# The first projection unit computed directly from x as it lands, sums of x formed in place by VectorE, cache copies issued in the FFN

## The chip, the cores and the metric

The kernel runs on one core of a Trainium2 chip. The metric is device time in microseconds of one execution of the whole program. Before the change the median of three runs is 2027.93 us (2026.84 to 2028.01). The engines named in the rows are PE (TensorE matmuls) and PEld (TensorE weight loads), DVE (VectorE), ACT (ScalarE), POOL (GpSimd) and SP (SyncE, which issues the DMAs).

## The reference, cut to what matters

One layer of a decoder trunk: a prompt of 1024 rows and 8 sample rows go through the same weights. All branches begin with one projection of x, and at the end stands a SwiGLU.

```python
z = x @ w_in
xr, yr, q, k, v, xq, g = jnp.split(z, SPLIT_IDX, axis=-1)
xc, conv_new = causal_conv(xr, conv_buf, conv_w, conv_b)
hs, h_new = rg_lru(xc, h0, lru_wa, lru_ba, lru_wx, lru_bx, lru_lambda)
a_out = hs * jax.nn.gelu(yr, approximate=True)
...
s_out, wk_new, wv_new = swa_decode(q, k, v, win_k, win_v, sinks)
c_out = mem_attn(xq.reshape(B, T, N_XHEADS, XHEAD_DIM), mem_k, mem_v)
gates = jax.nn.sigmoid(g.reshape(B, T, N_BRANCH, D_MODEL) + b_gates)
merged = sum(gates[:, :, n] * (br @ w_branch[n]) for n, br in enumerate((a_out, s_out, c_out)))
h = layer_norm(ALPHA * x + merged @ w_out, ln1_g, ln1_b)
gt, up = jnp.split(h @ w_gate_up, 2, axis=-1)
h = layer_norm(ALPHA * h + (jax.nn.silu(gt) * up) @ w_down, ln2_g, ln2_b)
```

`wk_new` and `wv_new` are the window caches of the sample rows: 127 old rows of each of 8 caches and one new row. The kernel makes the old rows' part by two copies from DRAM to DRAM, o_swk and o_swv.

## The kernel before, in words

**Layout.** Activations are held transposed: features on the 128 partitions, 1032 columns of rows (1024 of the prompt, 8 of the sample). Every matmul is exact to nearly f32 by a split: a value is written as hi plus lo, both in the fp32r type, and a product is three matmuls (hi by hi, hi by lo, lo by hi). The split of a tile is one cast on ACT (line 71, or 77 with a factor) and one subtraction on DVE (line 72, or 78).

**The projection.** 30 units, listed in UNITS ("xq" 0, "lru" 0, "gate" 0, "xq" 1, "lru" 1, ...), each make two blocks of 128 columns of z. A unit is computed by a Strassen-Winograd scheme: the 2 by 2 blocks of weights (two column blocks, two halves of D) and the 2 by 2 blocks of x (two halves of D, two halves of the rows) are combined into seven products instead of eight. Each product i is done for two halves p of its columns, 258 columns each, over 4 k steps with 3 matmuls each, so a unit is 168 matmuls. In the rows u_ih and u_il are hi and lo of the weight operand of product i, th and tl those of the x operand; products 0, 2, 4 and 6 go to the bank ub, 1 and 5 to ud, 3 to uc. The sums of weights (us, line 228) and their splits are made per unit by `fast_quarter`. The seven x operands are the same for all units and are made once, by `combos` (lines 161 to 208), while unit 0 runs: blocks of x are loaded one after the other (x<-xQ, eight DMAs of 516 KB), the four combinations for p = 0 are formed by DVE and those for p = 1 by POOL (line 180), each into a tile of its own, and all seven are split. Product i of unit 0 can start when operand i is ready.

`project` (lines 287 to 323) walks through all products of all units, calls `fast_quarter` three products ahead, and after each product `pump`, which moves side work one step on: the decode cross-attention of the sample rows (`dec_mem`, one per xq unit, pumped at every second call) and the lru branch. `dec_mem` loads tiles dck of the memory keys (two buffers) and the broadcast queries dcq (two buffers), multiplies and reduces them on DVE (dcj, line 757), and later sums values with the weights (dcv, dcw, line 781). It starts from `Finish.done` of its xq unit, which scales z, splits it (za, zb, hi_xq, lines 336 and 337) and stores it. The lru side work casts the convolved rows (xc to xch and xcl, lines 71 and 72) and runs small gate matmuls (g, lines 105 to 107).

**The cache copies.** `dec_win_scores`, late in the projection's program text, issues o_swk and o_swv (lines 809 to 811). A scheduler places them at build time; in the trace they are issued at 29 and 60 us.

**The FFN.** For each block f of 128 hidden columns, gate weights wfg and up weights wfu are loaded in two halves each (wfg3r, wfu3r: raw halves of block 3; line 82), split by ACT and DVE, and multiplied in three column chunks c = 0, 1, 2 (384, 384 and 264 columns) into fg and fu. Then ft = tanh(fg/2), ft = (ft + 1) fg, ft = ft fu (line 1041), and ft is split into gH and gL.

**What sets the order.** The program is a sequence of calls; a list scheduler at build time fixes one order of instructions for each engine from its own estimates of durations, and inserts the semaphore waits. On the chip each engine takes its instructions strictly in that order, so an instruction that waits holds up everything behind it on its engine. `tc.issue_after(x)` makes a DMA stand behind instruction x. Tile pools give the buffers out in turn: z has 9 buffers of 128 x 1032, "t" 28 buffers for x operands, "qh" 5 for weight his.

Of the kernel before, what the change touches and what calls it, by code (L numbers as in the profile page):

```python
# [10 lines left out]
F32 = mybir.dt.float32  # L11
F32R = mybir.dt.float32r
AF = mybir.ActivationFunctionType
ALU = mybir.AluOpType
# [4 lines left out]
P = 128  # L19
D = 1024  # L20
# [3 lines left out]
T = TP + NB  # L24
# [8 lines left out]
BANKS = {"mm": 3, "s": 2, "t": 2, "o": 1}  # L33
HT = T // 2
QN = T // 4
QS = 272
UNITS = (
    ("xq", 0), ("lru", 0), ("gate", 0), ("xq", 1), ("lru", 1), ("gate", 1), ("xq", 2), ("lru", 2), ("gate", 2),
    ("xq", 3), ("lru", 3), ("gate", 3), ("k", 0), ("lru", 4), ("v", 0), ("q", 0), ("lru", 5), ("gate", 4),
# [14 lines left out]
class Builder:  # L54
# [89 lines left out]


    def zt(self, name):
        return self.z.tile([P, T], F32, tag="z", name=name, bufs=9)

    def x_quarter(self, kh, th, p):

# [1 line left out]
        self.x_loaded = self.nc.sync.dma_start(t, self.io["xQ"][kh, 2 * th + p]).ins  # L152
        return t

    def combos(self, load, quarter):


        nc = self.nc
        ts = [[None] * 7, [None] * 7]
        for i in reversed(range(7)):  # L160
            for p in range(2):
                ts[p][i] = tuple(self.tp.tile([P, 4, QS], F32R, tag="t", name=f"t{e}{i}_{p}", bufs=28) for e in "hl")
        raw, t = [{}, {}], [{}, {}]

        def keep(i, p, src, sign=1.0):
            hi, lo = (a[:, :, :QN] for a in ts[p][i])
# [6 lines left out]
        def fetch(*where):  # L173
            for p in range(2):
                for kh, th in where:
                    raw[p][kh, th] = self.x_quarter(kh, th, p)

        def both(op, name, p, a, b):
            t[p][name] = self.zt(f"{name}_{p}")
            (nc.gpsimd if p else nc.vector).tensor_tensor(t[p][name], a, b, op)  # L180

        load(0)
        quarter(0)
        fetch((0, 0))
        for p in range(2):
            keep(0, p, raw[p][0, 0])
        load(1)
        quarter(1)
        fetch((0, 1))
        for p in range(2):  # L190
            both(ALU.subtract, "t1", p, raw[p][0, 0], raw[p][0, 1])
            keep(1, p, t[p]["t1"])
        fetch((1, 1))
        quarter(2)
        for p in range(2):
            both(ALU.subtract, "t3", p, raw[p][1, 1], raw[p][0, 1])
            both(ALU.add, "t2n", p, t[p]["t3"], raw[p][0, 0])
            keep(2, p, t[p]["t2n"], -1.0)
        load(3)
        fetch((1, 0))  # L200
        for p in range(2):
            keep(3, p, raw[p][1, 0])
        for p in range(2):
            keep(4, p, t[p]["t3"])
            keep(5, p, raw[p][1, 1])
            both(ALU.subtract, "t4", p, t[p]["t2n"], raw[p][1, 0])
            keep(6, p, t[p]["t4"])
        return ts

    def fast_load(self, u, src0, src1):  # L210
# [77 lines left out]
    def project(self):  # L288

        nc, io, tc = self.nc, self.io, self.tc  # L290
        self.qdc = self.cst.tile([P, KT * NB], F32, name="qdc")
        self.qds = self.cst.tile([P, KT * NB], F32, name="qds")
        self.kd = self.cst.tile([P, 2 * NB], F32, name="kd")
        self.vd = self.cst.tile([NB, 256], F32, name="vd")
        self.lru_setup()
        self.side, self.pumped = (deque(), deque()), 0
        n = len(UNITS)
        finish = [Finish(self, kind, j) for kind, j in UNITS]
        st = {}

        def load(u):
            a, b = finish[u].rows
            st[u] = self.fast_load(u, io["win"][a], io["win"][b])
            if u:
                st[u]["load"]((0, 0), (0, 1), (1, 0), (1, 1))

        load(0)
        parts = {0: ((0, 0),), 1: ((1, 0), (1, 1)), 3: ((0, 1),)}
        ts = self.combos(lambda i: st[0]["load"](*parts[i]), lambda i: self.fast_quarter(st[0], i))
# [491 lines left out]
    def dec_win_scores(self):  # L801

        nc, io, dp = self.nc, self.io, self.dp
        krow = dp.tile([NB, 256], F32, tag="krow", name="krow", bufs=1)
        ps = self.bank("mm", "dkt")
        for m in range(2):
            nc.tensor.transpose(ps[:NB, m * P:(m + 1) * P], self.kd[:, m * NB:(m + 1) * NB], self.ident)
        nc.scalar.copy(krow, ps[:NB, :256])
        for name, cache, row in (("o_swk", "cwk", krow), ("o_swv", "cwv", self.vd)):
            with self.tc.issue_after(self.last_mm):  # L810
                nc.sync.dma_start(io[name][:, 0:P - 1, :], io[cache][:, 1:P, :])
# [218 lines left out]
    def ffn(self, h):  # L1030
        nc, io, ph = self.nc, self.io, self.ph

        def gate_up(f, c, wg, wu, j):
            t0, n = CH[c]
            pg = self.mm_tile(wg, h, c, f"fg{f}_{c}", tag=("s", "t")[c % 2])
            self.norm_step()
            t = ph.tile([P, 384], F32, tag="gt", name=f"ft{f}_{c}", bufs=3)[:, :n]
            nc.scalar.activation(t, pg, AF.Tanh, scale=0.5)  # L1038
            nc.vector.scalar_tensor_tensor(t, t, 1.0, pg, op0=ALU.add, op1=ALU.mult)  # L1039
            pu = self.mm_tile(wu, h, c, f"fu{f}_{c}")  # L1040
            nc.vector.tensor_mul(t, t, pu)  # L1041
# [236 lines left out]
```

## Time and profile before

| | before |
|---|---|
| median of 3 runs | 2027.93 us |
| profiled execution, its span | 2027.6 us |
| PE busy in the span | 1963.3 us (97%), 13732 matmuls |
| DVE busy | 1204.2 us (59%) |
| ACT busy | 879.1 us (43%) |
| POOL busy | 125.3 us (6%) |
| DMA | 235.41 MB, mean 116 GB/s |
| mean granted TensorE clock | 0.991 |
| first 50 us: PE busy, granted clock | 29.98 us, 0.86 |
| 50 to 130 us: PE busy, granted clock | 71.81 us, 0.96 |

The profile is of one execution; its own time is the span, 2027.6 us, 0.3 us under the median. A row of the timeline reads: start, duration, engine, line, operation, output from inputs, count, and in brackets how long the engine had been idle before it and what released it. Matmul durations overlap, since matmuls are pipelined; the distance between starts is the pace.

### The profile page before, as it was taken

To read this page: it belongs to the slowest core of one execution; us is meant where nothing else is said; L and a number is where in the kernel's file an instruction comes from. 1 tells how busy PE (TensorE), PEld (TensorE's weight loads), DVE (VectorE), ACT (ScalarE), POOL (GpSimd) and SP (SyncE) were. 2 spreads that over 40 slices of the span, in tenths; PEclk is the share of its full clock that TensorE was granted. 3 is DMA by queue.
4 is the path that set the end of the run, shared out by engine and by line. 5 is a ranking of instruction groups with operands and counts; after the bars stand their busy time and mean duration, and the time that the engine had idled before them with its cause. 6 is when DMAs were issued, how large, how long until landed. Compare 5 with 4: busy or idle time off the path is not lost.

```text
span 2027.6 us, 35380 instructions
## 1 busy us (share of the span) xinstructions
PE 1963.3 (97%) x13732; PEld 1930.0 (95%) x13732; DVE 1204.2 (59%) x2565; ACT 879.1 (43%) x1922; POOL 125.3 (6%) x164
## 2 busy tenths in 40 slices
PE   6899999999999999999999999999999999999997
PEld 5899999999999898988999999999999999999996
DVE  8597888777676555389886568533322332223357
ACT  5456565555656455388774244422201221122324
POOL 3000010100000000012110003100000000000001
PEclk8999999999999999999999999999999999999999
DMA  4365455462333676567525241111211111111102
GB/s 173 129 227 181 153 186 170 144 228 82 118 131 114 234 240 215 158 170 204 155 72 174 85 145 30 43 42 43 58 47 43 42 57 41 57 45 43 56 28 84
DMA packets 140439, 235.41 MB, mean 116 GB/s; under 512 B 17280, under 2 KB 69584, under 8 KB 140240
## 3 DMA queue, kind: packets, MB, share of 16 engines
q1 hardware_dynamic: 140272, 233.17, 36.2%
q8 instruction: 107, 1.75, 0.4%
q14 instruction: 60, 0.49, 0.1%
HBM read 179.95 MB, written 55.23 MB: 116 GB/s over the span
## 4 chain that ended last, share of the span: by engine, by line
PE 86%; DVE 6%; DMA 3%; ACT 3%; issue 1%; SPq 0%; ACTq 0%; DVEq 0%; POOL 0%; POOLq 0%
PE ub L245 5%; PE ub L244 5%; PE ub L246 5%; PE fg L105 4%; PE fg L106 4%; PE fg L107 4%; PE fu L107 4%; PE fu L105 4%; PE fu L106 4%; PE d L105 3%; PE d L107 3%; PE d L106 3%; PE ud L246 2%; PE ud L245 2%; PE ud L244 2%; PE brs L105 1%
## 5 line engine op out<-in xcount | busy, mean ns | idle before, releaser
L105 PE MATMUL fg<-hH,wfg_h 128*128 128x384 f32 (+1 forms) x528 | 168.3, 319 | 3.0 <-DVE acc L1012 1.7
L106 PE MATMUL fg<-hL,wfg_h 128*128 128x384 f32 (+1 forms) x528 | 167.7, 318 | 0.4 <-DVE hL L1023 0.4
L107 PE MATMUL fu<-hH,wfu_l 128*128 128x384 f32 (+1 forms) x528 | 167.7, 318 | 0.0
L106 PE MATMUL fu<-hL,wfu_h 128*128 128x384 f32 (+1 forms) x528 | 167.6, 317 | 0.0
L105 PE MATMUL fu<-hH,wfu_h 128*128 128x384 f32 (+1 forms) x528 | 167.5, 318 | 0.0
L107 PE MATMUL fg<-hH,wfg_l 128*128 128x384 f32 (+1 forms) x528 | 167.5, 317 | 0.0
L1041 DVE TENSOR_TENSOR ft<-ft,fu 128x384 f32<-128x384 f32 (+1 forms) x66 | 33.8, 513 | 139.1 <-PE fu L107 139.1
L105 PE MATMUL d<-gH,wd_h 128*128 128x384 f32 (+1 forms) x360 | 114.4, 318 | 0.0
L106 PE MATMUL d<-gL,wd_h 128*128 128x384 f32 (+1 forms) x360 | 114.2, 317 | 0.0
L107 PE MATMUL d<-gH,wd_l 128*128 128x384 f32 (+1 forms) x360 | 114.2, 317 | 0.0
L1039 DVE SCALAR_TENSOR_TENSOR ft<-ft,fg 128x384 f32<-128x384 f32 (+1 forms) x66 | 33.8, 513 | 135.2 <-ACT ft L1038 132.9
L71 ACT CAST gH<-ft 128x384 fp32r<-128x384 f32 (+1 forms) x66 | 31.7, 481 | 175.0 <-DVE ft L1041 175.0
L105 PEld LDWEIGHTS fg<-hH,wfg_h 128*128 128x128 f32 x528 | 99.1, 188 | 3.9 <-DVE acc L1012 2.0
L106 PEld LDWEIGHTS fg<-hL,wfg_h 128*128 128x128 f32 x528 | 99.2, 188 | 1.0 <-DVE hL L1023 0.9
L107 PEld LDWEIGHTS fg<-hH,wfg_l 128*128 128x128 f32 x528 | 99.3, 188 | 0.0
L107 PEld LDWEIGHTS fu<-hH,wfu_l 128*128 128x128 f32 x528 | 99.2, 188 | 0.0
L105 PEld LDWEIGHTS fu<-hH,wfu_h 128*128 128x128 f32 x528 | 99.2, 188 | 0.0
L106 PEld LDWEIGHTS fu<-hL,wfu_h 128*128 128x128 f32 x528 | 99.2, 188 | 0.0
L1061 DVE SCALAR_TENSOR_TENSOR acc<-d,acc 128x384 f32<-128x384 f32 (+1 forms) x48 | 24.8, 516 | 108.4 <-PE d L107 108.4
L1038 ACT ACTIVATE ft<-fg 128x384 f32<-128x384 f32 (+1 forms) x66 | 30.1, 456 | 134.8 <-PE fg L107 134.8
L244 PE MATMUL ub<-th,u_0h 128*128 128x258 f32 x240 | 69.4, 289 | 7.5 <-ACT th L71 6.1
L244 PE MATMUL ud<-th,u_1h 128*128 128x258 f32 x240 | 70.2, 293 | 6.3 <-ACT u_1h L71 5.2
(957 smaller groups left out, 6872.4 us busy)
## 6 DMA issues: line engine op xcount, KB each, us to landing
ur<-win SPq DMA_DIRECT2D x120, 256.0 KB, 3.6
dck<-cmk SPq DMA_DIRECT2D x32, 256.0 KB, 3.6
dcv<-cmvT SPq DMA_DIRECT2D x32, 256.0 KB, 4.5
st<-scr_q SPq DMA_DIRECT2D x32, 256.0 KB, 5.2
scr_g<-za SPq DMA_DIRECT2D x12, 516.0 KB, 5.8
scr_g<-zb SPq DMA_DIRECT2D x12, 516.0 KB, 3.7
x<-xQ SPq DMA_DIRECT2D x8, 516.0 KB
scr_a<-ge SPq DMA_DIRECT2D x8, 516.0 KB
```

The lines of the kernel that those rows point to most:

```text
L71: ins = self.nc.scalar.copy(hi, src).ins
L105: nc.tensor.matmul(ps, sh, mh, start=i == 0, stop=False)
L106: nc.tensor.matmul(ps, sh, ml, start=False, stop=False)
L107: self.last_mm = nc.tensor.matmul(ps, sl, mh, start=False, stop=closes and i == last).ins
L244: mm(sh[:, w], xh, start=opens and k == 0, stop=False)
L245: mm(sh[:, w], xl, start=False, stop=False)
L246: self.last_mm = mm(sl[:, w], xh, start=False, stop=k == 3).ins
L1038: nc.scalar.activation(t, pg, AF.Tanh, scale=0.5)
L1039: nc.vector.scalar_tensor_tensor(t, t, 1.0, pg, op0=ALU.add, op1=ALU.mult)
L1041: nc.vector.tensor_mul(t, t, pu)
L1061: nc.vector.scalar_tensor_tensor(a, ps, 0.5, a, op0=ALU.mult, op1=ALU.add)
```

## The change

**The first unit.** Unit 0 is no longer done by seven products. `begin` takes the place of `combos`. It loads the unit's weights undivided (four halves), and the eight blocks of x in the order in which they are needed, and computes z of unit 0 block by block: for each quarter of the rows (th, p) it splits the two blocks of x of that quarter and multiplies them by both column blocks, 4 times 48 = 192 matmuls into the banks ub ("mm") and ud ("t"), which ACT then copies to za and zb.

**The x operands.** The splits of three blocks of x, made for unit 0, are used again as operands 0, 3 and 5 of the later units. The other four are formed in place, in the tiles of x, by DVE for p = 0 and p = 1 (three `change` calls in `begin` before operands 1 and 2, one before operand 6, for each p); POOL forms none. The z pool has 10 buffers instead of 9, and the "t" tiles 264 columns a row instead of 272.

**What follows.** `finish.done` of unit 0 (its scaling, split and store, and the start of its `dec_mem`) is called from `begin`; the seven-product units are 1 to 29.

**The cache copies.** o_swk and o_swv leave `dec_win_scores` and are issued in the FFN, behind the load of wfu of block 2 and of block 4.

```diff
-QS = 272
+QS = 264
...
-        return self.z.tile([P, T], F32, tag="z", name=name, bufs=9)
+        return self.z.tile([P, T], F32, tag="z", name=name, bufs=10)
...
-    def combos(self, load, quarter):
...
-        def both(op, name, p, a, b):
-            t[p][name] = self.zt(f"{name}_{p}")
-            (nc.gpsimd if p else nc.vector).tensor_tensor(t[p][name], a, b, op)
...
+    def begin(self, rows, finish, load_next, next_quarter):
...
+        def weight(j, e):
+            raw = self.half_raw(io["win"][rows[j]][:, e * h:(e + 1) * h], h, f"ur0_{j}{e}")
+            if e == 0:
+                w[j] = [None, None, pair(f"w{j}")]
+            flat = [a.rearrange("p k n -> p (k n)")[:, e * h:(e + 1) * h] for a in w[j][2]]
+            w[j][e] = flat
+            return lambda: self.split(*flat, raw)
...
+        def quarter(th, p, z):
+            tags = ("mm", "t")
+            for kh in range(2):
+                xh, xl = (a[:, :, :QN] for a in hl[kh, th, p])
+                for j in range(2):
+                    if kh == 0:
+                        ps[j] = self.bank(tags[j], f"u0{th}{p}{j}")[:, :QN]
+                    wh, wl = w[j][kh]
+                    for k in range(4):
+                        c, first, last = slice(k * P, (k + 1) * P), kh + k == 0, kh == 1 and k == 3
+                        nc.tensor.matmul(ps[j], wh[:, c], xh[:, k, :], start=first, stop=False)
+                        nc.tensor.matmul(ps[j], wh[:, c], xl[:, k, :], start=False, stop=False)
+                        self.last_mm = nc.tensor.matmul(ps[j], wl[:, c], xh[:, k, :], start=False, stop=last).ins
+            for j in range(2):
+                nc.scalar.copy(z[j][:, cols(th, p)], ps[j])
+
+        def change(op, p, to, a, b):
+            nc.vector.tensor_tensor(x[(*to, p)], x[(*a, p)], x[(*b, p)], op)
+            return x[(*to, p)]
...
+        for th, p in ((0, 1), (1, 0), (1, 1)):
+            block(0, th, p)
+            block(1, th, p)
+            quarter(th, p, z)
+            if (th, p) == (1, 0):
+                load_next()
+                next_quarter(0)
         for p in range(2):
...
+            ts[p][0], ts[p][3], ts[p][5] = hl[0, 0, p], hl[1, 0, p], hl[1, 1, p]
+            change(ALU.subtract, p, (1, 1), (1, 1), (0, 1))
+            ts[p][1] = keep(f"1_{p}", change(ALU.subtract, p, (0, 1), (0, 0), (0, 1)))
+        next_quarter(1)
         for p in range(2):
...
+            ts[p][2] = keep(f"2_{p}", change(ALU.add, p, (0, 0), (1, 1), (0, 0)), -1.0)
+        next_quarter(2)
+        finish.done(*z)
         for p in range(2):
...
+            ts[p][4] = keep(f"4_{p}", x[1, 1, p])
         for p in range(2):
...
+            ts[p][6] = keep(f"6_{p}", change(ALU.subtract, p, (1, 0), (0, 0), (1, 0)))
         return ts
...
-        todo = [(u, i) for u in range(n) for i in range(7)]
+        todo = [(u, i) for u in range(1, n) for i in range(7)]
...
-        for name, cache, row in (("o_swk", "cwk", krow), ("o_swv", "cwv", self.vd)):
-            with self.tc.issue_after(self.last_mm):
-                nc.sync.dma_start(io[name][:, 0:P - 1, :], io[cache][:, 1:P, :])
+        for name, row in (("o_swk", krow), ("o_swv", self.vd)):
             nc.sync.dma_start(io[name][:, P - 1, :], row)
...
+                if f in (2, 4):
+                    name, cache = (("o_swk", "cwk"), ("o_swv", "cwv"))[f // 2 - 1]
+                    with self.tc.issue_after(self.last_load):
+                        nc.sync.dma_start(io[name][:, 0:P - 1, :], io[cache][:, 1:P, :])
```

The scheduler's orders of the two programs differ on PE, DVE and ACT in the first ten or so units of the projection, and in the FFN only around blocks 3 and 5. Three places matter below. In these rows a tile has its number behind its name, and a line number counts in its own program (72 is in both the subtraction of a split).

The first place is DVE while operands of x are made. Before, in unit 0, the combinations of p = 0 (line 180) stand between the splits of operands (tl) and of unit 0's weights (u_4l, u_5l):

```order
L180 TENSOR_TENSOR t_0_184<-x_174,x_162 128x1032
L72 TENSOR_TENSOR u_4l<-us_4_304,u_4h 128x512
L180 TENSOR_TENSOR t2n_186<-t_0_184,x_144 128x1032
L228 TENSOR_TENSOR us_5_340<-us_2_178,ur_01_196 128x512
L228 TENSOR_TENSOR us_1_438<-ur_10_300,ur_11_302 128x512
L78 SCALAR_TENSOR_TENSOR tl_0_127<-t2n_186,th_0_126 128x4x258
L72 TENSOR_TENSOR u_5l<-us_5_340,u_5h 128x512
L78 SCALAR_TENSOR_TENSOR tl_1_129<-t2n_192,th_1_128 128x4x258
L180 TENSOR_TENSOR t_0_210<-t2n_186,x_198 128x1032
L72 TENSOR_TENSOR tl_0_123<-x_198,th_0_122 128x4x258
```

Now, behind the scaling of unit 0's z, the last sums in place (line 204) and the splits of operands 4 and 6 stand ahead of the first weight split of unit 1's product 3 (u_3l); nsnk and lruc are small constants:

```order
L72 TENSOR_TENSOR tl_0_447<-x_132,th_0_446 128x4x258
L72 TENSOR_TENSOR tl_1_451<-x_136,th_1_450 128x4x258
L204 TENSOR_TENSOR x_122<-x_114,x_122 128x1032
L204 TENSOR_TENSOR x_128<-x_126,x_128 128x1032
L72 TENSOR_TENSOR tl_0_456<-x_122,th_0_455 128x4x258
L72 TENSOR_TENSOR tl_1_461<-x_128,th_1_460 128x4x258
L660 TENSOR_SCALAR lruc<-vec 128x8
L72 TENSOR_TENSOR u_3l<-ur_01_330,u_3h 128x512
L789 SCALAR_TENSOR_TENSOR dcj_0_0_550,dcs_545<-dck_0_548,dcq_0_546 128x256
L789 SCALAR_TENSOR_TENSOR dcj_0_1_552,dcs_545<-dck_0_548,dcq_0_546 128x256
L263 TENSOR_TENSOR us_4_562<-ur_00_328,ur_10_332 128x512
```

What moved: the sums of p = 1, which POOL made before, now stand on DVE beside those of p = 0 (x_122 and x_128 here are the two for operand 6), and u_3l stands behind them and behind all splits of x.

The second place is DVE at the start of the unit behind the first lru unit. Before, the splits of the lru rows (xcl_1, xcl_2) and four products of the decode attention (dcj) stand ahead of the unit's first weight sums (us_1, us_2) and of u_1l:

```order
L72 TENSOR_TENSOR xcl_1_1054<-xc_792,xch_1_1053 128x344
L276 TENSOR_TENSOR za_943<-ud_0_854,u2s_0_904 128x258
L72 TENSOR_TENSOR xcl_2_1188<-xc_792,xch_2_1187 128x344
L757 SCALAR_TENSOR_TENSOR dcj_0_0_685,dcs_521<-dck_0_683,dcq_0_681 128x256
L757 SCALAR_TENSOR_TENSOR dcj_0_1_687,dcs_521<-dck_0_683,dcq_0_681 128x256
L757 SCALAR_TENSOR_TENSOR dcj_0_0_754,dcs_521<-dck_0_752,dcq_0_681 128x256
L757 SCALAR_TENSOR_TENSOR dcj_0_1_756,dcs_521<-dck_0_752,dcq_0_681 128x256
L228 TENSOR_TENSOR us_1_1021<-ur_10_844,ur_11_846 128x512
L228 TENSOR_TENSOR us_2_1057<-us_1_1021,ur_00_840 128x512
L72 TENSOR_TENSOR u_1l<-us_1_1021,u_1h 128x512
```

Now us_1 and us_2 of that unit, and u_0l and u_1l, stand ahead of xcl_1 and xcl_2:

```order
L263 TENSOR_TENSOR us_1_1003<-ur_10_826,ur_11_828 128x512
L263 TENSOR_TENSOR us_2_1047<-us_1_1003,ur_00_822 128x512
L789 SCALAR_TENSOR_TENSOR dcj_0_0_1043,dcs_545<-dck_0_1041,dcq_0_1039 128x256
L263 TENSOR_TENSOR us_4_1141<-ur_00_822,ur_10_826 128x512
L72 TENSOR_TENSOR u_0l<-ur_00_822,u_0h 128x512
L789 SCALAR_TENSOR_TENSOR dcj_0_1_1131,dcs_545<-dck_0_1127,dcq_0_1039 128x256
L308 SCALAR_TENSOR_TENSOR zb_971<-ub_1_805,p5s_1_864 128x258
L72 TENSOR_TENSOR u_1l<-us_1_1003,u_1h 128x512
L263 TENSOR_TENSOR us_5_1181<-us_2_1047,ur_01_824 128x512
L72 TENSOR_TENSOR xcl_1_1036<-xc_776,xch_1_1035 128x344
L72 TENSOR_TENSOR xcl_2_1178<-xc_776,xch_2_1177 128x344
```

What moved is us_1, us_2 and u_1l: from behind both splits of lru rows to ahead of both.

The third place is ACT in the FFN at the passage from block 2 to block 3 (the passage from 4 to 5 reads alike). Before, three of the four casts of block 3's weights (wfg_h, wfu_h of wfg3r and wfu3r) stand ahead of the cast of block 2's last chunk (gH_2), and the fourth, not shown, still further ahead:

```order
L71 CAST gH_1_16734<-ft_1_16705 128x384
L71 CAST wfg_h<-wfg3r__16802 128x512
L71 CAST wfu_h<-wfu3r__16808 128x512
L1038 ACTIVATE ft_2_16763<-fg_2_16738 128x264
L71 CAST wfu_h<-wfu3r__16814 128x512
L71 CAST wfg_h<-wfg4r__16994 128x512
L71 CAST gH_2_16792<-ft_2_16763 128x264
L1038 ACTIVATE ft_0_16845<-fg_0_16820 128x384
```

Now all four stand behind it:

```order
L71 CAST gH_1_16723<-ft_1_16694 128x384
L1068 ACTIVATE ft_2_16752<-fg_2_16727 128x264
L71 CAST gH_2_16781<-ft_2_16752 128x264
L71 CAST wfg_h<-wfg3r__16785 128x512
L71 CAST wfg_h<-wfg3r__16791 128x512
L71 CAST wfu_h<-wfu3r__16797 128x512
L71 CAST wfu_h<-wfu3r__16803 128x512
L71 CAST wfg_h<-wfg4r__16983 128x512
L1068 ACTIVATE ft_0_16834<-fg_0_16809 128x384
```

The casts wfg3r and wfu3r moved from ahead of gH_2 of block 2 to behind it, together with the first cast of block 4.

More of the change, by code (lines that the diff above doesn't have):

```diff
@@ L153, in x_quarter, with keep @@
         return t
-    def combos(self, load, quarter):
[L158 to L166, printed above, removed]
+    def begin(self, rows, finish, load_next, next_quarter):
+        nc, io, h = self.nc, self.io, D // 2
+        pair = lambda name: tuple(self.tp.tile([P, 4, QS], F32R, tag="t", name=f"t{e}{name}", bufs=28) for e in "hl")
+        x, hl, ts, w, ps = {}, {}, [[None] * 7, [None] * 7], [[None] * 2, [None] * 2], {}
+        cols = lambda th, p: slice(HT * th + QN * p, HT * th + QN * (p + 1))
+        def weight(j, e):
[5 more added lines that the diff above has]
+            return lambda: self.split(*flat, raw)
+        def keep(name, src, sign=1.0):
+            tiles = pair(name)
+            hi, lo = (a[:, :, :QN] for a in tiles)
             src = src.rearrange("p (k n) -> p k n", k=4)
@@ L171, in keep, with fetch @@
                 self.split(hi, lo, src)
[L173 to L176, printed above, removed]
-        def both(op, name, p, a, b):
-            t[p][name] = self.zt(f"{name}_{p}")
[L180 to L184, printed above, removed]
+            return tiles
+        def fetch(kh, th, p):
+            x[kh, th, p] = self.x_quarter(kh, th, p)
@@ new lines, in block @@
+        def block(kh, th, p):
+            hl[kh, th, p] = keep(f"{kh}{th}{p}", x[kh, th, p])
+        def quarter(th, p, z):
[13 more added lines that the diff above has]
+                nc.scalar.copy(z[j][:, cols(th, p)], ps[j])
@@ new lines, in change @@
+        def change(op, p, to, a, b):
+            nc.vector.tensor_tensor(x[(*to, p)], x[(*a, p)], x[(*b, p)], op)
+            return x[(*to, p)]
+        s00 = weight(0, 0)
+        fetch(0, 0, 0)
+        s10, s01 = weight(1, 0), weight(0, 1)
+        fetch(1, 0, 0)
+        s11 = weight(1, 1)
+        for th, p in ((0, 1), (1, 0), (1, 1)):
+            fetch(0, th, p)
+            fetch(1, th, p)
+        z = self.zt("za0"), self.zt("zb0")
+        s00()
+        block(0, 0, 0)
+        s10()
@@ L185, in combos @@
+        s01()
+        block(1, 0, 0)
+        s11()
+        quarter(0, 0, z)
+        for th, p in ((0, 1), (1, 0), (1, 1)):
+            block(0, th, p)
[4 more added lines that the diff above has]
+                next_quarter(0)
         for p in range(2):
[L186 to L189, printed above, removed]
+            ts[p][0], ts[p][3], ts[p][5] = hl[0, 0, p], hl[1, 0, p], hl[1, 1, p]
+            change(ALU.subtract, p, (1, 1), (1, 1), (0, 1))
+            ts[p][1] = keep(f"1_{p}", change(ALU.subtract, p, (0, 1), (0, 0), (0, 1)))
@@ L199, in combos @@
-        load(3)
-        fetch((1, 0))
-        for p in range(2):
[L202 to L207, printed above, removed]
+            ts[p][4] = keep(f"4_{p}", x[1, 1, p])
+        for p in range(2):
+            ts[p][6] = keep(f"6_{p}", change(ALU.subtract, p, (1, 0), (0, 0), (1, 0)))
         return ts
@@ L303, in load @@
             st[u] = self.fast_load(u, io["win"][a], io["win"][b])
[L304 to L309, printed above, removed]
+            st[u]["load"]((0, 0), (0, 1), (1, 0), (1, 1))
+        ts = self.begin(finish[0].rows, finish[0], lambda: load(1), lambda i: self.fast_quarter(st[1], i))
         with tc.issue_after(self.x_loaded):
```

7 lines of the change are left out of this document (removed).

## The prediction

> **What bounds the kernel now.** I read the page first, then the windows of the stages that the change touches, then PE's waits there.
>
> ```profile
> PE 1963.3 (97%) x13732; PEld 1930.0 (95%) x13732; DVE 1204.2 (59%) x2565; ACT 879.1 (43%) x1922; POOL 125.3 (6%) x164
> 0.00:50.00 50.00, 29.98 (x182) 28.07 (x183) 43.57 (x62) 24.87 (x38) 17.27 (x16) 0.86 0.48 172
> 50.00:130.00 80.00, 71.81 (x559) 69.83 (x558) 53.62 (x136) 38.45 (x77) 0.32 (x2) 0.96 0.53 177
> 130.00:680.00 550.00, 543.64 (x4482) 541.28 (x4480) 422.55 (x833) 310.43 (x586) 33.09 (x39) 1.00 0.45 152
> 1290.00:1400.00 110.00, 110.00 (x707) 110.00 (x707) 36.14 (x66) 26.31 (x52) 0.05 (x1) 1.00 0.17 51
> ```
>
> In a window row stand the window, its length, busy us of PE, PEld, DVE, ACT, POOL with their instructions, PE's granted clock, DMA share and GB/s. PE is the bound with 97% of 2027.6 us; of its 64 us of idle time 20 lie in the first 50 us and 8 in the next 80, and only there is the granted clock below 1. DVE is busy for 43.57 of the first 50 us. In the FFN (the last row) PE has no gap at all: there the change can only lose. PE's waits in the first 130 us:
>
> ```profile
> PE ub L244 <- ACT th L71: 6.1, 1, 6.1
> PE ub L244 <- ACT th L77: 5.4, 1, 5.4
> PE ud L244 <- ACT u_1h L71: 5.2, 2, 4.5
> DVE xcl L72 <- ACT xch L71: 8.7, 3, 7.2
> DVE dcj L757 <- DMA dck<-cmk: 2.8, 3, 1.2
> ```
>
> (Total, times, longest.) The first 6.1 are the start, which stays. The 5.4 are unit 0 waiting for operand 2, which needs two sums of blocks. The longest of the 5.2 lies in unit 3 and answers to the last two rows, DVE's own waits: DVE stood 7.2 us for a row of lru work while the weights of unit 3 were queued behind it.
>
> **Paces.**
>
> ```profile
> 7.72 0.42 PE L246 MATMUL ub<-th,u_0l 128*128 128x258 f32 x1
> 11.38 0.37 PE L245 MATMUL ub<-tl,u_0h 128*128 128x258 f32 x1
> 16.73 0.58 PE L245 MATMUL ud<-tl,u_1h 128*128 128x258 f32 x1 [3.06 <-DVE tl L72]
> 36.13 0.39 PE L245 MATMUL uc<-tl,u_3h 128*128 128x258 f32 x1 [1.38 <-DVE tl L72]
> 36.48 0.28 PE L244 MATMUL uc<-th,u_3h 128*128 128x258 f32 x1
> 39.95 0.28 PE L246 MATMUL ud<-th,u_5l 128*128 128x258 f32 x1
> 68.72 0.28 PE L244 MATMUL ub<-th,u_0h 128*128 128x258 f32 x1
> 124.70 0.28 PE L244 MATMUL ub<-th,u_0h 128*128 128x258 f32 x1
> 144.98 0.28 PE L244 MATMUL ub<-th,u_0h 128*128 128x258 f32 x1
> ```
>
> From 7.72 to 11.38 are 17 steps of 0.215 us: cold. From 36.48 to 39.95 are 29 steps of 0.1197: warm. A cold spell lasts about 20 matmuls, 4.3 us, and costs 20 x 0.095 = 1.9 us. After 1.38 us of idle time (36.13) PE was warm; 3.06 (16.73) left it cold. The last three rows are the first matmuls of units 2, 4 and 5.
>
> **(a) Units 0 and 1: -10.8.** Before, they end at 68.72. After, the first two matmuls hang on the same first loads and casts; I keep 6.07 for the first and 7.34 for the second. The other 190 of the 192 are 20 x 0.215 + 170 x 0.12 = 24.7, so unit 0 ends at 32.0, if x comes in time:
>
> ```profile
> 0.00:16.00 16.00, 5.85 (x25) 5.15 (x25) 9.77 (x12) 8.32 (x11) 2.85 (x5) 0.97 0.84 312
> ```
>
> 312 GB/s over 16 us are 5.0 MB; unit 0 wants 8 x 516 KB and 4 x 256 KB, 5.2 MB, there by 16.8 us at that rate. The last two blocks are wanted when quarter 3 begins at 26.3, less 2.3 for cast and split: slack of some 7 us. Unit 1 then runs products 0 to 2 (72 matmuls, 8.6 us, and 0.3 for the small transposes of unit 0's decode columns) to 40.9, and wants u_3l of product 3. In the first order fence that stands behind the sums and splits of x on DVE. Its price:
>
> ```profile
> 18.94 3.43 DVE L180 TENSOR_TENSOR t<-x,x 128x1032 f32<-128x1032 f32 x1
> 18.50 2.78 POOL L180 TENSOR_TENSOR t<-x,x 128x1032 f32<-128x1032 f32 x1 [4.12 <-DVE tl L72]
> 26.80 0.68 DVE L228 TENSOR_TENSOR us<-ur,ur 128x512 f32<-128x512 f32 x1
> 37.53 1.23 DVE L72 TENSOR_TENSOR tl<-x,th 128x1032 fp32r<-128x1032 f32 x1
> 38.68 1.22 DVE L72 TENSOR_TENSOR tl<-t,th 128x1032 fp32r<-128x1032 f32 x1
> ```
>
> A full-width row of DVE takes 1.23 and starts 1.15 after the last (37.53 to 38.68); a row of 512 goes at 0.60. Beside POOL's sum the same work took 3.43; with POOL without sums I take 1.15. The last block of x is split at about 21.3: its cast stands on ACT behind the copy of quarter 1's first bank, at 19.1. From there DVE has, up to and with u_3l, 17 full-width rows (8 of them sums in place), 6 weight rows and 5 small ones of 0.08: 19.6 + 3.6 + 0.4 = 23.6, so 44.9. PE stands 3.5 to 4 us, long enough to go cold, and has 92 matmuls left: 20 x 0.215 + 72 x 0.12 = 12.9. Unit 1 ends at 57.9: -10.8.
>
> Bounds: without the stall 52.3 (-16.4). On the other side the first products of the decode attention (dcj) stand on DVE right behind u_3l and wait for dcq:
>
> ```profile
> 53.58 0.35 SPq L740 DMA_DIRECT2D dcq<-drow_c  x1
> 57.98 0.80 SPq L751 DMA_DIRECT2D dcq<-dcq  x2
> dcq<-dcq SPq DMA_DIRECT2D x16, 256.0 KB, 3.4
> ```
>
> 4.4 us from issue to issue and 3.4 to land: unit 0's z is split by 36.9, the issue comes at 37.6, dcq lands at 45.4, when DVE arrives. If it is late by 3.5, unit 1's u_4l and u_5l are late too: 61.5 (-7.2).
>
> **(b) Units 2 and 3: -12.5.** From 68.72 to 124.70 are 55.98 us; unit 4, undisturbed, takes 144.98 - 124.70 = 20.28. What fills the rest:
>
> ```profile
> 97.61 0.52 DVE L72 TENSOR_TENSOR xcl<-xc,xch 128x344 fp32r<-128x344 f32 x1 [7.23 <-ACT xch L71]
> L105 PE MATMUL g<-xch,wgh 128*128 128x344 f32 x6 | 2.1, 356 | 0.7 <-ACT xch L71 0.7
> dck<-cmk SPq DMA_DIRECT2D x32, 256.0 KB, 3.6
> ```
>
> xcl_2 (97.61) needs a cast that ACT makes behind the eviction of unit 3's product 0; behind xcl_2 stand us_1, us_2 and u_1l, without which product 1 cannot start. In the second order fence these three stand ahead of xcl_1 and xcl_2, and so DVE is some 7 to 9 us ahead of PE where it was behind. Without the jam the two units are 2 x 20.28 and 18 gate matmuls of 344 columns (six of each of three lines; 0.1197 x 344/258 = 0.16 each): 43.5, so -12.5. The wait for xcl goes on, with no weights behind it that PE wants at once. Bounds: -12.5 and 0 (the jam comes back, a rival).
>
> **(c) Units 4 to 10: +1.5.** The decode rows that the jam held back now fall a unit or so earlier beside others. The order leaves DVE 1 to 2 us ahead of PE in units 4 and 5; a few small waits like the three for dck (2.8 together) are the nearest row. I take half of that, bounds 0 and +4.
>
> **(d) FFN blocks 3 and 5: +4.1.**
>
> ```profile
> 1332.70 0.34 PE L105 MATMUL fg<-hH,wfg_h 128*128 128x384 f32 x1
> 1332.90 0.43 DVE L1041 TENSOR_TENSOR ft<-ft,fu 128x264 f32<-128x264 f32 x1 [0.77 <-PE fu L107]
> 1333.36 0.41 ACT L71 CAST gH<-ft 128x264 fp32r<-128x264 f32 x1
> 1328.39 0.62 ACT L71 CAST wfg_h<-wfg3r__16802 128x512 fp32r<-128x512 f32 x1 [0.23 <-PE fg L106]
> 1330.04 0.69 DVE L72 TENSOR_TENSOR wfg_l<-wfg3r__16802,wfg_h 128x512 fp32r<-128x512 f32 x1 [0.68 <-issue]
> ```
>
> PE began block 3 at 1332.70, right behind block 2. In the third order fence the casts of block 3 stand behind gH_2, which needs ft of the last chunk. ft ends at 1333.33, gH at 1333.77, the first wfg_h at 1334.4: PE starts 1.7 late, and after two matmuls waits 0.4 more for wfg_l (0.69). That is 2.05 a passage, twice 4.1. The later halves come in time: a cast takes 0.62, a half of fg (12 matmuls of 384 columns) about 2.0. Bounds: 3.2 (the second wait hidden) and, if each gap makes the clock cold, 4.1 + 2 x 1.9 = 7.9. The gap of 1.38 that stayed warm is nearer than the 3.06 that did not.
>
> By the Trainium skill ("TensorE: Matmul & The Clock Gate", in Part 1 under "What's actually happening") the array falls to half clock only after a whole idle window of about 3.4 us, and comes back after about 3.4 us of sustained work. The warm start after 1.38 us agrees; the cold spell of 4.3 us at 7.72 is longer than that figure. By the rule (d) is 4.1 and its upper bound falls away.
>
> **(e) The copies: 0.**
>
> ```profile
> 29.08 0.91 SPq L811 DMA_DIRECT2D o_swk<-cwk  x1
> 30.00:32.00 2.00, 2.00 (x11) 2.00 (x11) 2.00 (x3) 1.16 (x3) 0.24 (x1) 0.50 1.21 401
> 1290.61 0.33 SPq L82 DMA_DIRECT2D wfg3r__16802<-wgu  x1
> ```
>
> One copy is 1 MB read and 1 MB written, some 5 us at 401 GB/s, and fell beside loads that nothing waited for at that moment. In the FFN the DMA share is 0.17, and block 3's weights were issued at 1290.61, 38 us ahead of their cast at 1328.39. Without that lead it would cost the 5 us.
>
> **The sum.** -10.8 - 12.5 + 1.5 + 4.1 = -17.7, against the span of 2027.6: 2009.9. The median is 0.3 above the span: 2010.2, so 2010. The bounds of the terms added up give 2002 to 2020.
>
> **Rivals.** *The jam comes back in another unit* (chance 0.17): the same rows exist, DVE at 20.11 of 20.3 us was full in unit 4:
>
> ```profile
> 124.70:145.00 20.30, 20.30 (x171) 20.19 (x170) 20.11 (x40) 12.80 (x20) 2.29 (x3) 1.00 0.64 220
> ```
>
> Then (b) is nothing: 2010 + 12.5 = 2022.5. Against it speaks the same row: PE lost nothing in that unit, though DVE was full.
>
> *Unit 0 is bound by x* (0.04): were the loads as slow as the mean of the first 50 us (172 GB/s), 5.2 MB would be in at 30.6, and the last quarter would end near 30.6 + 1.05 + 1.2 + 5.7 = 38.5 instead of 32: 2016.5. The first window speaks against it.
>
> *Slower: the ring of dck buffers stalls DVE* (0.07). There are two dck buffers; each of the first unit's 6 reloads waits for DVE's dcj of two tiles before, then takes 0.4 to issue and 3.6 to land. If DVE meets each too early it loses 6 x 4 = 24 us, of which some 8 are slack, and 4 more at dcq: +20 on 2010, so 2030, slower than before. It decides where the DVE work between a release and the next use falls under 4 us; by the order it is 6.7, 6, over 8, 9, 4.4 and 3.3, so only the last two are tight.
>
> **How the numbers follow.** The forecast has 0.72, the rivals 0.17, 0.04 and 0.07. Its own range is 2003 to 2020; with the jam it goes to 2023, and some 0.18 lies outside 2003 to 2023. A measurement tells 0.2%, 4 us, from no change. Faster by more than that (under 2023.9): nearly all of the forecast (0.71), most of the jam's case (0.13), x (0.04): 0.88; the rest of the jam's case is the same, 0.04; slower 0.08.
>
> **What would show it.** (a) The first matmul of the second seven-product unit (ub from u_0h) near 58, one wait of PE for u_3l of some 3.5 us, none for x operands ("th L77", 5.4) any more, POOL nearly idle in the first 50 us; (b) DVE's wait for xch without a wait of PE for u_1h; 43 to 44 us for two units; (d) two gaps of PE of about 2 us in the FFN, each ended by ACT's cast of wfg, at full clock; (e) no wait for wfg or wfu raw halves. It is wrong if a unit of 2 to 6 takes 30 us, if PE waits for x in unit 0, or if dcj waits for dck by more than some 8 us in all.

## The result, and the profile after

The changed kernel takes 2013.47 us (median of 4 runs, 2010.85 to 2014.40) against 2027.74 for the kernel before: a ratio of 0.9928 (95% interval 0.9915 to 0.9940), 14 us faster. A second comparison, with 5 runs of it, gave 2013.62 (2008.77 to 2016.91) and the same ratio (0.9914 to 0.9941). The forecast was 2010, range 2003 to 2023.

The page's first lines of the kernel after:

```profile
span 2011.5 us, 35413 instructions
PE 1962.2 (98%) x13756; PEld 1929.8 (96%) x13756; DVE 1197.3 (60%) x2558; ACT 878.9 (44%) x1921; POOL 112.4 (6%) x160
PEclk9999999999999999999999999999999999999999
```

PE is busy for nearly as long as before (1963.3): of the 16.1 us between the spans 15 are idle time that went. The windows of the same stages (columns as in the prediction), and two stretches of 2 us in the FFN:

```profile
0.00:50.00 50.00, 38.99 (x289) 38.46 (x290) 41.32 (x61) 31.67 (x50) 2.81 (x12) 0.97 0.60 219
50.00:130.00 80.00, 79.20 (x652) 78.76 (x652) 68.66 (x167) 44.15 (x84) 4.66 (x7) 1.00 0.50 172
1290.00:1400.00 110.00, 106.82 (x660) 105.76 (x659) 30.72 (x56) 22.04 (x44) 0.00 (x0) 0.98 0.15 51
1314.00:1316.00 2.00, 2.00 (x13) 2.00 (x12) 0.89 (x2) 0.44 (x1) 0.00 (x0) 1.00 1.00 355
1362.00:1364.00 2.00, 2.00 (x8) 2.00 (x8) 0.00 (x0) 0.00 (x0) 0.00 (x0) 0.51 0.80 294
```

In the first 50 us PE is busy for 38.99 instead of 29.98, in the next 80 for 79.20 instead of 71.81, at a clock of 0.97 and 1.00 instead of 0.86 and 0.96. The FFN stage, without a gap before, now has 3.2 us of them. Behind the first gap, at 1312, the clock stays at 1.00, and a cache copy's 355 GB/s pass beside PE unnoticed; behind the second, at 1359, it is 0.51. Of PE's waits the largest that are new, and DVE's waits of the first 160 us that answer to those shown of before:

```profile
PE uc L281 <- DVE u_3l L72: 4.1, 1, 4.1
PE fg L105 <- ACT wfg_h L71: 3.0, 2, 1.5
DVE xcl L72 <- ACT xch L71: 1.3, 2, 1.1
DVE dcj L789 <- DMA dck<-cmk: 1.2, 3, 0.5
```

The wait for operand 2 (5.4) and that for u_1h (5.2) are gone; so is the 7.2 us wait of DVE for xch. The landmarks of PE's timeline after: the end of the stall in unit 1, the first matmuls of units 2, 4 and 5, and of FFN blocks 3 and 5:

```profile
46.18 0.39 PE L281 MATMUL uc<-th,u_3l 128*128 128x258 f32 x1 [4.11 <-DVE u_3l L72]
58.84 0.28 PE L279 MATMUL ub<-th,u_0h 128*128 128x258 f32 x1
102.40 0.28 PE L279 MATMUL ub<-th,u_0h 128*128 128x258 f32 x1
122.56 0.28 PE L279 MATMUL ub<-th,u_0h 128*128 128x258 f32 x1
1312.40 0.44 PE L105 MATMUL fg<-hH,wfg_h 128*128 128x384 f32 x1 [1.49 <-ACT wfg_h L71]
1359.50 0.44 PE L105 MATMUL fg<-hH,wfg_h 128*128 128x384 f32 x1 [1.48 <-ACT wfg_h L71]
```

Against 68.72 and 124.70 before, PE is 9.9 us ahead at unit 2 and 22.3 at unit 4. It enters the FFN 21.9 ahead (first fg at 1241.61 instead of 1263.54), loses 2.1 at block 3 and 3.7 at block 5, and keeps 16.1 to the end.

### The profile page after: what moved, and what is told of

It reads as the page before. It is cut to its first block, busy times and chain, and to the rows that moved or that the text cites. A ratio compares the mean times of both kernels' runs of the same rounds, so it can differ in the third digit from the quotient of the medians.

```text
span 2011.5 us, 35413 instructions
## 1 busy us (share of the span) xinstructions
PE 1962.2 (98%) x13756; PEld 1929.8 (96%) x13756; DVE 1197.3 (60%) x2558; ACT 878.9 (44%) x1921; POOL 112.4 (6%) x160
## 4 chain that ended last, share of the span: by engine, by line
PE 70%; ACT 4%; DVE 3%; DMA 3%; issue 1%; SPq 0%; ACTq 0%; POOL 0%; DVEq 0%; POOLq 0%
PE fg L107 4%; PE fg L105 4%; PE fg L106 4%; PE fu L107 4%; PE fu L105 4%; PE fu L106 4%; PE d L105 3%; PE d L107 3%; PE d L106 3%; PE ub L279 2%; PE ub L281 2%; PE ub L280 2%; PE brs L105 2%; PE brs L106 2%; PE brs L107 1%; PE bra L106 1%
## 5 line engine op out<-in xcount | busy, mean ns | idle before, releaser
L565 ACT ACTIVATE bp<-bp,bst 128x257 f32<-128x257 f32 (+1 forms) x128 | 62.8, 493 | 18.1 <-DVE bst L561 18.0
L281 PE MATMUL uc<-th,u_3l 128*128 128x258 f32 x232 | 66.4, 287 | 4.1 <-DVE u_3l L72 4.1
```

What stands on the lines that cost most here:

```text
L281: self.last_mm = mm(sl[:, w], xh, start=False, stop=k == 3).ins
L565: nc.scalar.activation(x, x, AF.Exp, bias=st[:, g:g + 1], scale=-1.0, accum_out=st[:, 4 + g:5 + g])
```

## The experiments

Two theories were to be told apart first. **A**: the jam of units 2 and 3 belonged to the cache copies, because the scheduler, reckoning with their transfer time, placed loads and weight sums late; in the FFN the same reckoning puts the weight casts late (the runs can show what the copies' place does to the order, not how the scheduler reckons). **B**: the direct unit 0 cured the jam, and the copies only cost at the FFN.

**e1: the copies back in their old place.** The rest of the change stays.

```diff
-        for name, row in (("o_swk", krow), ("o_swv", self.vd)):
+        for name, cache, row in (("o_swk", "cwk", krow), ("o_swv", "cwv", self.vd)):
+            with self.tc.issue_after(self.last_mm):
+                nc.sync.dma_start(io[name][:, 0:P - 1, :], io[cache][:, 1:P, :])
...
-                if f in (2, 4):
```

> The changed kernel with the two cache copies back in their old place (issued early in the projection); unit 0 stays direct. Theory A: the jam of units 2 and 3 (DVE waiting for xcl with the weights of the next unit queued behind) belongs to the copies, since their transfer time makes the scheduler place the loads and weight sums of those units late; by the order, xcl_1 and xcl_2 stand ahead of us_1, us_2 and u_1l of a unit again. Then the jam's 12.4 us come back and the 5.8 us of the two FFN gaps go: 2013.5 + 12.4 - 5.8 = 2020, units 2 and 3 together near 56 us. Rival B: the jam is cured by the direct unit 0 (decode work starts earlier); then only the FFN gaps go: 2013.5 - 5.8 = 2007.7, units 2 and 3 near 43.5 us.

Measured: 2020.12 us (median of 5, 2013.43 to 2022.21), 0.9956 of the kernel before (0.9941 to 0.9971), as A has it; B's 2007.7 lies outside all runs. The waits of DVE and of PE, from 58 to 125 us, and the FFN window:

```profile
DVE xcl L72 <- ACT xch L71: 8.7, 3, 7.2
PE ud L279 <- ACT u_1h L71: 3.1, 2, 2.4
1290.00:1400.00 110.00, 110.00 (x704) 110.00 (x703) 34.75 (x64) 25.19 (x49) 0.00 (x0) 1.00 0.14 49
```

DVE's wait of before is back to the tenth, though unit 0 is direct, and the FFN has no gap. Units 2 and 3 take 53.5 us (58.25 to 111.78), not the 56 of A: the profile is of the run of 2013.43, the quickest of the five. In it three gate matmuls fall into PE's wait in unit 3 (PE stands 1.0 us for xch and 2.4 for u_1h, 4.5 for u_1h before), and PE's later wait for dcj (1.5 before) is absent. What the other four runs lost beyond it no trace shows.

**e2: the copies moved, nothing else.** The kernel before, with only the last two pieces of the diff.

> The kernel before with one part of the change alone: the cache copies issued in the FFN at blocks 2 and 4; unit 0 by seven products, POOL sums as before. Theory A (the copies make the jam): 2027.7 - 12.4 + 5.8 = 2021, no wait of PE for u_1h in unit 3, units 2 and 3 near 43.5 us after a first matmul of unit 2 at 68.7. Rival B (the direct unit cures it): 2027.7 + 5.8 = 2033.5, units 2 and 3 near 56 us.

Measured: 2020.99 us (2018.01 to 2024.79), 0.9965 (0.9952 to 0.9978). Unit 2 starts at 68.67 as before, unit 4 at 112.04: 43.4 us, the jam is gone without the direct unit. The second window and the FFN's waits:

```profile
50.00:130.00 80.00, 80.00 (x662) 79.77 (x661) 64.91 (x158) 44.33 (x86) 3.13 (x5) 1.00 0.59 196
PE fg L105 <- ACT wfg_h L71: 3.0, 2, 1.5
```

So A holds as to the copies' place, and B falls. The medians nearly add up: the direct unit alone (e1) is worth 7.9 us of the 2028.05 beside it, the copies alone (e2) 7.1, both together 14.3.

**e3: the copies in 16 pieces.** Is it the order of the casts or the transfer that makes the FFN's gaps?

```diff
-                if f in (2, 4):
-                    name, cache = (("o_swk", "cwk"), ("o_swv", "cwv"))[f // 2 - 1]
+                if f < 16:
+                    (name, cache), b = (("o_swk", "cwk"), ("o_swv", "cwv"))[f // 8], f % 8
                     with self.tc.issue_after(self.last_load):
-                        nc.sync.dma_start(io[name][:, 0:P - 1, :], io[cache][:, 1:P, :])
+                        nc.sync.dma_start(io[name][b:b + 1, 0:P - 1, :], io[cache][b:b + 1, 1:P, :])
```

> The changed kernel with each copy cut into 8 pieces of 127 KB, one issued in each of the FFN blocks 0 to 15; same bytes. By the order the casts of blocks 3 and 5 stand ahead of gH_2 again and the projection is that of the changed kernel. Theory A (the gaps come from the order of the casts, not from the transfers): no gap of PE at the passages, 2013.5 - 5.8 = 2007.7, and less spread between runs. Rival C (the transfer itself delays the weights): gaps stay, spread over more blocks, 2013 or more.

Measured: 2005.96 us (2004.96 to 2006.26), 0.9892 (0.9875 to 0.9908). The same window of the FFN:

```profile
1290.00:1400.00 110.00, 110.00 (x708) 110.00 (x707) 35.56 (x65) 25.82 (x50) 0.00 (x0) 1.00 0.16 51
```

The bytes move as before, and the gaps are gone. Pieces make the single transfer shorter too, so by itself this run does not part order from transfer; the changed kernel's own trace does:

```profile
1268.62 0.52 SPq L82 DMA_DIRECT2D wfg3r__16785<-wgu  x1
1311.42 0.41 ACT L71 CAST gH<-ft 128x264 fp32r<-128x264 f32 x1 [2.93 <-DVE ft L1071]
1311.74 0.61 ACT L71 CAST wfg_h<-wfg3r__16785 128x512 fp32r<-128x512 f32 x1
```

Block 3's weights were issued 43 us ahead of their cast, and the cast followed without a pause on gH, for which ACT had stood 2.93 us: it was the order. From the first matmul of fg to the start of its last chunk the FFN takes 659.3 us, as in the kernel before, against 665.1 in the changed one. The runs lie within 1.3 us, those of the changed kernel within 3.6 in the first comparison and 8.1 in the second; as e10, which has no such gap either, spreads over 8.6, the gaps are not shown to make the spread.

**e4: a copy at each even block from 2 to 20.** Written again with the same bytes, to make more gaps.

```diff
-                if f in (2, 4):
-                    name, cache = (("o_swk", "cwk"), ("o_swv", "cwv"))[f // 2 - 1]
+                if f % 2 == 0 and 2 <= f <= 20:
+                    name, cache = (("o_swk", "cwk"), ("o_swv", "cwv"))[f // 2 % 2 == 0]
```

> The changed kernel with a copy at each even block from 2 to 20 (o_swk and o_swv in turn, written again with the same bytes). By the order all four casts stand behind gH_2 at blocks 3, 5, 7, 11, 13, 19 and 21, three of them at 17 and one at 9. It asks what a gap of 1.5 us does to the clock: in the changed kernel the one at block 3 left it full, the one at block 5 brought 0.64 and 0.51 for 4 us. Theory D (where the gap falls decides): some of the gaps go cold, some don't, each whole passage costs 2.1 or 3.7 to 4, 5 to 6 more of them 11 to 23 us: 2024 to 2037. Rival E (a gap of that length stays warm, the one at block 5 had another cause): 2.1 each, 2024 to 2026, no further cold spell.

Measured: 2026.78 us (median of 8, 2023.71 to 2029.78). The profile is of the quickest run; its FFN waits and one window:

```profile
PE fg L105 <- ACT wfg_h L71: 10.4, 7, 1.5
PE d L105 <- ACT wd_h L71: 1.5, 1, 1.5
1300.00:1400.00 100.00, 96.82 (x617) 95.76 (x616) 30.16 (x55) 20.75 (x42) 0.00 (x0) 1.00 0.19 64
```

Seven gaps of 1.48 us, none of them cold: by itself this profile speaks for E. But its time is the lower end of a range of 6 us, and five other profiles with the two gaps (after, its second comparison below, e2, e5, e6) each show one gap that went cold and one that stayed warm; that of e8 shows two warm. In all 5 of the 19 gaps of 1.48 to 1.49 us ahead of an fg went cold (e4's one of 1.49 ahead of d did not). 36 matmuls from the end of a gap take 6.74 us when warm and 8.3 when cold: a cold one costs 1.6. As D has it, gaps of one length end both ways; that their place decides is not shown. Nor does the length decide alone: the gap of 1.68 to 1.83 us ahead of the FFN's first block stayed warm in all 13 profiles.

**e5: unit 1's u_3 split early.** On DVE u_3l moves from the 44th to the 32nd row.

```diff
         next_quarter(2)
+        next_quarter(3)
         finish.done(*z)
...
-            if k + ahead < len(todo):
+            if 0 < k < len(todo) - ahead:
```

> The changed kernel with the weights of unit 1's product 3 (u_3h, u_3l) split ahead of the scaling of unit 0's z and of operands 4 and 6; by the order u_3l moves from the 44th to the 32nd row of DVE. Theory F (DVE's whole amount ahead of product 4 is the bound, u_3l only its first victim): the stall of 4.1 us moves to u_4l, which stands behind the same work and behind the first decode rows: stall at 43.8 to about 48.3, unit 2 starts again near 58.8, time 2013 (2011 to 2015). Rival G (u_3l's place alone): no stall, unit 2 starts at 52.7, 2013.5 - 6 = 2007.5.

Measured: 2013.59 us (2009.82 to 2015.78), 0.9929 (0.9910 to 0.9949): nothing won. PE's wait in unit 1, and the cast that ended it:

```profile
PE ub L280 <- ACT u_4h L71: 3.6, 1, 3.6
48.80 0.62 ACT L71 CAST u_4h<-us 128x512 fp32r<-128x512 f32 x1 [1.32 <-DVE us L264]
```

The cast itself waited for DVE's sum us. The stall moved on by one product, as F has it. It was not the place of u_3l but DVE's amount of work ahead of it. (Unit 1 to unit 2 takes 26.75 us here, 26.28 in the changed kernel.)

**e6: what may wait, behind what may not.** Products 3 to 5's weights and operand 4 ahead of unit 0's scaling and split, operand 6 last.

```diff
         next_quarter(2)
-        finish.done(*z)
+        next_quarter(3)
         for p in range(2):
             ts[p][4] = keep(f"4_{p}", x[1, 1, p])
+        next_quarter(4)
+        next_quarter(5)
+        finish.done(*z)
...
-            if k + ahead < len(todo):
+            if 2 < k < len(todo) - ahead:
```

> The changed kernel with, in unit 1, the weights of products 3 to 5 and operand 4 ahead of the scaling of unit 0's z, and that ahead of operand 6. By Theory F nothing that products 3 and 4 need stands behind work that can wait: u_3l near 36, operand 4 near 37, u_4l near 39 (needed at 43.8), operand 6 near 47 (needed at 49.6). No stall, no cold spell: unit 2 starts at about 52.7 instead of 58.8, 2013.5 - 6 = 2007.5. Rival H (the decode chain now starts later and DVE meets dcq too early, with u_6l and unit 2's weights behind): a stall of 3 to 6 us at product 6 or in unit 2, 2011 to 2014.

Measured: 2009.55 us (2008.29 to 2012.91), 0.9916 (0.9901 to 0.9931). The stall before product 3 is gone, but PE has another one:

```profile
51.86 0.68 DVE L72 TENSOR_TENSOR u_0l<-ur,u_0h 128x512 fp32r<-128x512 f32 x1
52.60 0.39 PE L284 MATMUL ub<-th,u_0l 128*128 128x258 f32 x1 [1.95 <-DVE u_0l L72]
```

The scheduler had put unit 2's first matmuls ahead of unit 1's product 6; u_0l came 1.95 us late, and from 53.7 to 57.0 PE ran cold (0.50 in the window from 55 to 57). Unit 2's other matmuls start at 57.57, 1.3 us earlier than in the changed kernel, not 6; the profiled run wins another 1.9 from there to the FFN, without a cause that was tested. H named the place (unit 2's weights), but not the cause: DVE shows no wait for dcq here, it was busy from 28 to 58 us.

**e7: e3 and e6 together.**

> The edits of e3_pieces and e6_reorder together: no gap in the FFN, no stall in unit 1. If both theories hold the gains add: 2013.5 - 5.8 - 6 = 2001.7 (2000 to 2004). If one fails, 2007 to 2008.

Measured: 2005.05 us (2002.08 to 2006.21), 0.9889 (0.9874 to 0.9903); the same stall (1.96 us at 53.20). The FFN's gain is there, but the time is not to be told from e3's: e6's gain does not come on top.

**e8: the sums of p = 1 on POOL.**

```diff
-            nc.vector.tensor_tensor(x[(*to, p)], x[(*a, p)], x[(*b, p)], op)
+            (nc.gpsimd if p else nc.vector).tensor_tensor(x[(*to, p)], x[(*a, p)], x[(*b, p)], op)
```

> The changed kernel with the in-place sums of p = 1 on POOL instead of DVE. Theory I (POOL's sums stretch DVE's rows beside them, as in the kernel before, where 1.23 became 3.4): DVE is rid of 4 rows of 1.15 but four others take about 2.2 more, and operand 1 of p = 1 comes 2 to 3 us later: the stall before product 3 grows by 2 to 4 us, 2015 to 2018. Rival J (DVE is simply relieved): u_3l 4 us earlier, stall gone, 2007 to 2009.

Measured: 2015.46 us (2012.33 to 2017.71), 0.9941 (0.9926 to 0.9957); the interval overlaps that of the changed kernel, but unit 2 starts at 61.38 instead of 58.84. POOL's first two sums, the DVE row beside them, and the waits of ACT and PE:

```profile
21.82 6.16 POOL L204 TENSOR_TENSOR x<-x,x 128x1032 f32<-128x1032 f32 x2 [21.40 <-DMA ur<-win]
22.26 3.44 DVE L204 TENSOR_TENSOR x<-x,x 128x1032 f32<-128x1032 f32 x1
ACT th L77 <- POOL x L204: 4.9, 1, 4.9
PE drt_c L770 <- ACT qdc L1203: 6.8, 2, 4.9
```

J falls. I's time came out, but not by its path: DVE's row is stretched to 3.44 as I has it, yet the price is paid elsewhere: ACT waits 4.9 us for POOL's second pair of sums with the cast of operand 2 (th, line 77), and that pair began only at 34.47, behind eight small copies of POOL (scvo, from 27.91); behind the cast stands qdc, and PE waits 6.8 us for qdc (drt_c, the transposes of unit 0's decode columns). u_3l is then only 0.2 late.

**e9: unit 0's scaling behind unit 1.** e7, with `finish.done` of unit 0 out of `begin`.

```diff
-        finish.done(*z)
+        self.z0 = z
...
             self.fast_step(st[u], i, ts, finish[u])
+            if k == 6:
+                finish[0].done(*self.z0)
             self.pump()
```

> The kernel with the copies in pieces and the reordered begin, and the scaling, split and store of unit 0's z (with the start of its decode work) moved behind unit 1's last product. In the reordered kernel the stall before product 3 was gone, but DVE, busy without a gap from 28 to 58 us, made u_0l of unit 2 at 51.9 instead of the 50.4 at which PE wanted it: a gap of 1.95 us and a cold spell, so unit 2 ended up 1.3 us earlier than in the changed kernel and not 6. Theory F (DVE's amount is the bound; whatever may wait must leave): 2.3 us of split and 2 us of decode rows leave the stretch, u_0l comes 3 to 4 us earlier, no gap, no cold spell: unit 2 some 4 us earlier, 2005.1 - 4 = 2001. Rival K (the work moved falls into units 2 to 4, where DVE has no slack either): 2004 to 2007.

Measured: 1999.07 us (1998.52 to 1999.72), 0.9858 (0.9844 to 0.9871), the best median here and 14 us better than the change (6 of them against e7). Unit 2, and the two windows:

```profile
52.73 0.37 PE L282 MATMUL ub<-th,u_0h 128*128 128x258 f32 x1
0.00:50.00 50.00, 43.06 (x339) 42.53 (x340) 41.43 (x64) 31.85 (x50) 2.90 (x12) 1.00 0.53 190
50.00:130.00 80.00, 78.81 (x651) 78.51 (x651) 69.74 (x166) 46.06 (x89) 6.73 (x7) 1.00 0.55 184
```

52.73 against 58.84: 6.1 us, about the stall of 4.1 and its cold spell, and F holds (it had forecast 4). The clock is at 1.00 in both windows.

**e10: the lru constants behind unit 1 as well.**

```diff
-        self.lru_consts()
         todo = [(u, i) for u in range(1, n) for i in range(7)]
...
                 finish[0].done(*self.z0)
+                self.lru_consts()
```

> The same with the some 26 small rows that make the lru constants (0.08 us each, 2 us in all) also moved behind unit 1. Theory F: the stall is gone already, so nothing more is won: as the last one, within 1 us. If the last one still had a gap, this one closes it. Rival K: the constants are wanted by the first lru unit and now come 2 to 4 us late: 1 to 3 us slower than the last one.

Measured: 1999.60 us (1994.57 to 2003.12), 0.9856 (0.9837 to 0.9875): as e9, since no gap was left. Unit 2 starts at 53.28.

**The changed kernel again**, beside e9 and e10:

> The changed kernel itself, to be compared on the same chip: 2013.5, between 2010.5 and 2015, depending on whether none, one or both of the gaps at blocks 3 and 5 go cold (1.6 us each).

Measured: 2013.62 us (2008.77 to 2016.91), a wider spread than the 3.2 us of two cold spells would explain.

## Why the prediction was right, and where it was off

| term | predicted | measured |
|---|---|---|
| (a) units 0 and 1 | -10.8 | -9.9 |
| (b) units 2 and 3 | -12.5 | -12.4 |
| (c) from unit 4 to the FFN | +1.5 | +0.4 |
| (d) FFN blocks 3 and 5 | +4.1 | +5.8 |
| (e) the copies' own transfers | 0 | 0 (e3) |
| span | 2009.9 | 2011.5 |

**(a)** The direct unit is not bound by x: PE waits 0.9 us for a weight cast and then for nothing until unit 1 at 32.56 (predicted 32.0). PE stood 4.11 us for u_3l, predicted 3.5 to 4, then ran cold (0.54 from 48 to 50 us). The walk along DVE's order began at the split of x's last block and ended with u_3l:

```profile
21.22 1.29 DVE L72 TENSOR_TENSOR tl<-x,th 128x1032 fp32r<-128x1032 f32 x1 [0.78 <-ACT th L71]
45.44 0.69 DVE L72 TENSOR_TENSOR u_3l<-ur,u_3h 128x512 fp32r<-128x512 f32 x1
```

From the end of the first (22.51) to that of the second (46.13) are 23.6 us, as predicted; what was late is the start, 22.5 instead of 21.3, and that is about what the term lacks. e5 corrects the wording: the stall was laid to u_3l's place, but what binds is all of DVE's work ahead of product 4. It makes no difference to the sum, but it does to the cure (e6, e9).

**(b)** 43.56 us for the two units, predicted 43.5: the price was right because it was taken from the undisturbed unit 4. But the prediction saw only that the rows had changed places and did not ask which edit moved them. e1 and e2 show that it was the copies' move, which (e) priced at 0. Their transfers do cost nothing; what the copies cost before is the order that came with their old place. So the sum holds the gain, but the prediction did not know which edit earned it.

**(c)** That this term came within 1.1 is luck. In the stretch that it names, units 4 to 10, PE won 0.5 us (128.6 against 129.1). From unit 10 to the last it lost 4.1, 3.0 of it in idle time (4.6 against 1.5; the longest wait, 1.72 us at 424.15, is for v, which PE transposes into vt), and the stage from there to the FFN won 3.3; the term names neither. The other kernels here differ by 1 to 4 us in the same stretches, and the cause was not tested; this stays open.

**(d)** is the term that was mis-sized. Each gap was right (1.49 and 1.48 plus a slow start; block 3, which stayed warm, lost 2.1, predicted 2.05). The choice was that such a gap stays warm, from the one row of before with 1.38 us; the second one went cold and cost 1.6 more, the 0.51 in the window above. 5.8 lies inside the bounds of 3.2 to 7.9. The Trainium skill ("TensorE: Matmul & The Clock Gate", in Part 1 under "What's actually happening") has the array fall to half clock after a whole idle window of about 3.4 us; here 5 of 19 gaps of 1.5 us were enough. The measurement decides: a gap of that length can end either way.

**The median** was set 0.3 above the span. The profiled run itself took 2013.24, 1.7 above its span of 2011.5. Of the 3.5 us between forecast and median, 1.6 come from the terms, 1.4 from this step, and 0.2 are the median's distance from the profiled run; the rest is rounding. Every run here whose span is on record took 1.7 to 3.1 us more than its span, so the 2027.6 of before is a span and not, as the part on the time before has it, that execution's own time.

**The rivals.** The jam did not come back: none of units 2 to 10 takes more than 22.6 us. e1 shows on what it hangs, the copies in their old place; the rival looked for it in DVE's load. x did not bind unit 0. The ring of dck buffers cost DVE 1.2 us of waits in the first 160 and 4.2 in the whole run (6.5 before), not 24.

**One reading** was too wide: the clock before is below 1 not only in the first 130 us. From 680 to 688, behind PE's wait of 5.0 us for baH, it is 0.57; in the changed kernel that spell comes too (0.50 from 662 to 664), so the sum is not touched.

## What to carry to other kernels

Where a scheduler fixes the order from its own estimates, price a moved DMA also by the order that it leaves behind and the order that it makes at the new place: here two transfers that cost nothing themselves were worth 12.4 us in one stage and minus 5.8 in another, and cutting them into 16 pieces kept the one and avoided the other (2005.96). When a stall follows from an engine that is busy throughout, moving its victim forward only moves the stall by one product (e5); what helps is to take work that can wait out of the stretch altogether (e9, 1999.07).

## What the runs showed of the hardware

Gaps of PE of one length, 1.48 to 1.49 us, at the same passage of the same loop, are followed by full clock in 14 cases and by a cold spell in 5, with 0.51 granted in the window of 2 us shown and 1.6 us lost. A gap of 1.95 us (e6) went cold too, about 1 us after it had ended, and so did one of 1.79 (e2, ended at 180.42, clock 0.50 from 182 to 184). But those of 1.68 to 1.83 us at the start of the FFN stayed warm in all 13 profiles, and so did one of 2.11 (before, ended at 914.29, clock 1.00 from 914 to 918): between 1.5 and 2.1 us the length alone does not decide. And the sum that took DVE 3.43 us beside POOL's before took 3.44 beside POOL's in e8, and 1.22 alone: in these rows the in-place form makes no difference.
